# A hybrid conv/attention/mixture-of-experts block: the overflow table moved into the conditional block, twelve expert units in place of thirteen, and each unit's down projection one unit later

## The chip, the cores and the metric

The kernel runs on one core of a Trainium2 chip. The metric is the device time of one execution in microseconds (us); the figure to predict is the median of several runs. Besides those runs, one execution was profiled, and every row below comes from that one.

## The reference, cut to what matters

One layer on 512 tokens of width 1024, all in float32. The first half (convolution module, latent attention, output projection) is not touched by the change. The second half is a mixture of 32 experts; each token goes to two of them:

```
def hier_moe(h, w_group, b_group, w_expert, b_expert, w_gate_e, w_up_e, w_down_e):
    ...                                  # top group of 4, top 2 experts of its 8, weights "gates"
    y = jnp.zeros_like(h)
    for e in range(N_EXPERTS):           # 32; w_gate_e[e], w_up_e[e]: 1024 x 256, w_down_e[e]: 256 x 1024
        a = jax.nn.silu(h @ w_gate_e[e]) * (h @ w_up_e[e])
        y = y + gates[:, e:e + 1] * (a @ w_down_e[e])
    return y
```

Each expert has 3 MB of weights, so all 32 have 96 MB. The tokens that each expert gets follow from the inputs. Counted with the reference's own draw (seed 0), expert 5 has 87 tokens, the next four have 57, 53, 53 and 50, and 512 x 2 = 1024 rows are spread over the 32.

## The kernel before, in words

**Units.** The experts are worked off in units. A unit holds 128 rows of gathered tokens. The string `ORDER = "eeellsllsolss"` gives the sequence. An `e` unit has two experts fixed beforehand (experts 0 to 5 in three units), with 64 rows each. An `l` unit has two experts that are chosen at run time, by length, with 64 rows each; an `s` unit has four of the shorter ones with 32 rows each. The `o` unit has the first overflow: an expert with more tokens than rows is loaded again, for up to 64 more. Here expert 5 has 87 tokens and 64 rows, so its last 23 tokens are the `o` unit's. Further overflow would be worked off behind the units in nested conditional blocks (`over_body`, `nest`), which jump over their content when `n_over` is small.

**Tiles.** The weights of an expert come in three tiles of 1 MB: part 0 (half of the gate and up weights), part 1 (the other half), and part `d` (down). `load` issues them from SyncE's queue, in the order of the list `keys`: unit after unit, within a unit part 0 of all its experts, part 1, `d`. There are 33 x 3 = 99 tiles. `room` lists the free buffers: 4 of a ring (`r`) and 14 slots (`s`). So 18 tiles are loaded before the first unit runs; after that, each tile waits for a buffer that a unit gives back. SyncE's queue is in order: one tile whose buffer is not free holds all that come after it.

**A unit's steps.** `start` gathers the rows (an indirect DMA issued by POOL, two units ahead), transposes them on TensorE (L1443) and scales them. `gate_up` (L1467) multiplies by part 0 and then part 1. ACT and DVE make silu and product (L1470, L1472), `turn` transposes the result (L1479), `down` (L1492) multiplies by `d`; DVE scales with the routing weight (L1495), ACT rounds the high part (L1496), POOL takes the low part (L1497). `combine` (L1503, L1508) scatters the rows back to tokens by a matmul with a one-hot matrix (L1456) and adds them to the residual, for two units at once, eight groups of 512 columns by 128 tokens. The engines' orders are written out by hand: in each unit TensorE does `gate_up`, the next unit's transposes, part of a `combine`, `turn`, another part, `down`.

**Beside the units.** The first unit's rows are made without a gather, as a matmul (`first_unit`). Routing weights (`gates`) are computed behind the first unit's start. `scatter` then writes the overflow table to DRAM by eight indirect DMAs from POOL (L1319); `table` is filled beforehand. `over_table` makes the list of overflow blocks. The last unit's `part 1` and `d` tiles are cut in two and loaded alternately for two experts at a time.

Of the kernel before, what the change touches and what calls it, by code (L numbers as in the profile page):

```python
# [34 lines left out]
NSTAT, NLONG = 6, 10  # L35
# [5 lines left out]
def hybrid_block(ctx: ExitStack, tc: tile.TileContext, A, out, dbg=None, stop=None):  # L41
# [21 lines left out]
    NW, NSL = 4, 17  # L63
# [16 lines left out]
    tmp = ctx.enter_context(tc.tile_pool(name="tmp", bufs=6))  # L80
# [839 lines left out]
    ORDER = "eeellsllsolss"  # L920
# [47 lines left out]
    ahead, HOLD = [], 99  # L968
    UE, ULONG = NSTAT // 2, NLONG // 2
    UO = UE + ULONG + NSHORT // 4  # L970
    room = ["r"] * 4 + ["s"] * 14
# [5 lines left out]
    def load(key, n):  # L977

# [6 lines left out]
        if isinstance(e, int):  # L985
            pick = lambda w: w[e]
        else:
            if part == 0:
                src = oi[0:1, 0:1] if e is None else od[0:1, e[1]:e[1] + 1]
                reg_of[e] = sp.value_load(src, min_val=0, max_val=31)  # L990
            pick = lambda w: w[bass.ds(reg_of[e], 1)].rearrange("e p a b -> (e p) a b")
# [12 lines left out]
    def load_keys(ks):  # L1004

        first = len(Wt)
        for ds in zip(*[load(key, len(ks)) for key in ks]):
            for o, i in sum(ds, []):
                d = sp.dma_start(o, i)
                if first == HOLD:  # L1010
                    tc.add_manual_dep(d.ins, ahead[0].ins.name, sync, reason="order of the transfers")
                    first = None


    units = []
    keys = []
    for kind in ORDER:
        n_ = sum(k == kind for k, _, _ in units)
        if kind == "e":
            u_ = n_, [2 * n_, 2 * n_ + 1]  # L1020
        elif kind == "l":
            u_ = UE + n_, [("p", NSTAT + 2 * n_ + i) for i in range(2)]
        elif kind == "s":
            u_ = UE + ULONG + n_, [("p", NSTAT + NLONG + 4 * n_ + i) for i in range(4)]
        else:
            u_ = None, [None]
        ks = [[(e, part) for e in u_[1]] for part in (0, 1, "d")]
        keys += sum(ks if units else [ks[0], ks[2], ks[1]], [])
        units.append((kind, *u_))
    nxt = [0]  # L1030
    LAST = [(units[-1][2][i], part) for i in range(0, len(units[-1][2]), 2) for part in (1, "d")]

    def loads_upto(n):
        while room and nxt[0] < min(n, len(keys)):
            m = 2 if keys[nxt[0]] in LAST else 1
# [7 lines left out]
    rt = C([128, 2160], name="u", uname="rt")  # L1043
    rpos = [0]

    def R(shape, dt=F32):
# [5 lines left out]
        assert rpos[0] <= 2160  # L1052
# [34 lines left out]
    tfill = T([128, NROW // 128, 2])  # L1087
    dve.memset(tfill[:, :, 0], 1000.0)
    dve.memset(tfill[:, :, 1], 0.0)
    fill = pool.dma_start(table.rearrange("(p a) b -> p a b", p=128), tfill)  # L1090
    tokrow = R([512])
    iota(tokrow, [[1, 512]], 0)
    i4, i32, i64 = tokrow[:, :4], tokrow[:, :32], tokrow[:, :64]
# [9 lines left out]
    Vt = rt[:32, :128]  # L1103
    i32, e32 = tokrow[:, :32], tokrow[:32, :32]
    iota(ecol, [[0, 1]], 0, 1)
    dve.tensor_scalar(kbase[:, :NSTAT], e32[:, :NSTAT], -20000.0, 1e6, op0=OP.mult, op1=OP.add)
    dve.tensor_scalar(kbase[:, NSTAT:], e32[:, NSTAT:], -1.0, 31.0, op0=OP.mult, op1=OP.add)
# [39 lines left out]
    def route(tt):  # L1147
# [52 lines left out]
        dve.tensor_tensor(mr, M[:, 0, 0:2], M[:, 1, 0:2], op=OP.add)  # L1200
# [6 lines left out]
        dve.tensor_tensor(o, i64b, pk[:, 0:2, None].to_broadcast([128, 2, 64]), op=OP.is_equal)  # L1207
# [5 lines left out]
        hot = R([2, 64])  # L1213
        dve.tensor_tensor(hot, i64b, rk[:, :, None].to_broadcast([128, 2, 64]), op=OP.is_equal)
# [31 lines left out]
    def place(tt, o, r):  # L1246
# [4 lines left out]
        for k in range(2):  # L1251
            for h in range(2):
                pe.matmul(pst[0][64 * h:64 * h + 64, o:o + UE], hot[:, k, :], r[:, k, h:NSTAT:2],
# [3 lines left out]
    def by_expert(tt, o, r):  # L1257

        hot = routed[tt][-1]
        for k in range(2):  # L1260
            pe.matmul(pst[0][:32, 128 + o:192 + o], r[:, k, :], hot[:, k, :], start=False, stop=(tt == 3 and k == 1),
                      tile_position=(0, 0), skip_group_check=True)

    def by_unit(o):

        v = Vt[:, o:o + 64]
        for h in range(2):
            pe.matmul(pst[0][64 * h:64 * h + 64, 256 + o:256 + o + ULONG], v, perm[:, NSTAT + h:NSTAT + NLONG:2],
                      start=False, stop=True, tile_position=(0, 64 * h), skip_group_check=True)
        for i in range(4):  # L1270
            pe.matmul(pst[0][32 * i:32 * i + 32, 256 + o + ULONG:256 + o + UO - UE], v[:, :32], perm[:, NSTAT + NLONG + i::4],
                      start=False, stop=True, tile_position=(0, 32 * i), skip_group_check=True)

    def gates():
# [20 lines left out]

# [5 lines left out]
        for tt in range(4):  # L1301
            place(tt, 64, routed[tt][5])
            by_expert(tt, 64, routed[tt][5])
        dve.tensor_copy(sv[:, :UE, 1], pst[0][:, 64:64 + UE])
        dve.tensor_copy(Vt[:, 64:], pst[0][:32, 192:256])
        yield
        by_unit(64)
        dve.tensor_copy(sv[:, UE:UO, 1], pst[0][:, 320:320 + UO - UE])
        yield

    def rows_by_unit():
        by_unit(0)
        dve.tensor_scalar(sidx[:, UE:UO], pst[0][:, 256:256 + UO - UE], 1000.0, None, op0=OP.add)
        dve.tensor_scalar(sv[:, UE:UO, 0], pst[0][:, 256:256 + UO - UE], 1000.0, None, op0=OP.add)

    def scatter():
        for tt in range(4):
# [19 lines left out]
    for tt in range(4):  # L1337
# [5 lines left out]
        if tt < 3:  # L1343
            n = 31 + 8 * tt
            for d, f in ((0, lambda tt=tt: x2_part(tt, 1)), (D0, step), (D1, lambda step=step: step(2)), (D2 if tt < 2 else 8.5, step),
                         (D3 if tt < 2 else 11.5, places)):
                at(n + d, f)
    rows0 = chain(*[first_unit(tt) for tt in range(3)])
    last_rows = first_unit(3)
    for n, f in ((53, lambda: x2_part(3, 1)), (53, lambda: run(rows0, 2)), (55, lambda: x2_part(3, 2)), (55.1, step),  # L1350
                 (55.6, lambda: run(rows0, 1)), (55.8, step), (56, step), (56.1, lambda: run(rows0, 1)), (57, lambda: step(2)),
                 (58, lambda: run(rows0, 2)), (60, step), (61, lambda: run(last_rows)), (62, places)):
# [22 lines left out]
    dve.tensor_copy(Vt[:, :64], pst[0][:32, 128:192])  # L1375
# [4 lines left out]
    def over_table():  # L1380
        rpos[0] = 128
# [5 lines left out]
        dve.tensor_scalar(xn[:32, 4:5], place_of, NSTAT + NLONG - 0.5, 32.0, op0=OP.is_gt, op1=OP.mult)  # L1387
# [29 lines left out]
        ov = R([2 * NOVER + 1])  # L1417
        dve.tensor_copy(ov, pov[:, :2 * NOVER + 1])
        dve.tensor_scalar(ov[:, NOVER:2 * NOVER], ov[:, NOVER:2 * NOVER], NROW - 64.0, None, op0=OP.add)
        dve.tensor_copy(oi[:, :2 * NOVER + 1], ov)  # L1420
# [6 lines left out]
    class Unit:  # L1427
# [3 lines left out]
        def __init__(self, ne, tokf, gate, buf, weights, first=False):  # L1431
            self.ne, self.gate, self.buf, self.weights = ne, gate, buf, weights
            self.w = w = 32 if ne == 4 else 64
            n = self.n = w * ne
            self.hg = hg
            if first:
                act.copy(buf[:, :512], pg[0])
                dve.tensor_copy(buf[:, 512:], pg[1])
# [8 lines left out]
            self.rest = pt, tokf  # L1447

        def complete(self):
            pt, tokf = self.rest  # L1450
# [4 lines left out]
            self.ot = T((128, 512), F32R)  # L1455
            dve.tensor_scalar(self.ot[:n], tokrow[:n], tokf, None, op0=OP.is_equal)  # L1456

        def gate_up(self, between=None):
            n, wd_ = self.n, self.w
            gu = acc()  # L1460
            for j in range(8):
                if j == 4 and between:
                    between()
                for i in range(self.ne):
                    w = self.weights(i, j // 4)
                    sl = slice(wd_ * i, wd_ * i + wd_)
                    pe.matmul(gu[sl, :], self.hg[:, j, sl], w.t[:, :, j % 4, :],  # L1467
                              start=(j == 0), stop=(j == 7), tile_position=(0, wd_ * i), skip_group_check=True)
# [14 lines left out]
        def down(self, last=False):  # L1483
            n, wd_ = self.n, self.w
            self.yhl = S([128, 2, 1024], F32R)
            for hf in range(2):
                hs = slice(512 * hf, 512 * hf + 512)
                o = acc()
                for c in range(2):
                    for i in range(self.ne):  # L1490
                        w = self.weights(i, "d")
                        pe.matmul(o[wd_ * i:wd_ * i + wd_, :], self.aT[:, n * c + wd_ * i:n * c + wd_ * i + wd_], w.t[:, c, hs],  # L1492
                                  start=(c == 0), stop=(c == 1), tile_position=(0, wd_ * i), skip_group_check=True)
# [3 lines left out]
                (dve if last and hf else pool).tensor_tensor(self.yhl[:n, 1, hs], yf[:n], self.yhl[:n, 0, hs].bitcast(F32), op=OP.subtract)  # L1497

    def scattered(o, tt, hf, us, start, stop):

        for m, u_ in enumerate(us):
            for k in range(2):
                pe.matmul(o, u_.ot[:u_.n, tt * 128:(tt + 1) * 128], u_.yhl[:u_.n, k, 512 * hf:512 * hf + 512],  # L1503
                          start=start and m == 0 and k == 0, stop=stop and m == len(us) - 1 and k == 1)

    def add(o, tt, hf):
        xr = xrow(tt)[:, 512 * hf:512 * hf + 512]
        dve.tensor_tensor(xr, xr, o, op=OP.add)  # L1508
        return xr

    def combine(us):

        for tt in range(4):
            for hf in range(2):
                o = fb()
                scattered(o, tt, hf, us, True, True)
                add(o, tt, hf)
                yield

    def combine_last(before, last):  # L1520

        o = {}

        def first(tt, hf, bank):
            o[tt, hf] = bank()
            scattered(o[tt, hf], tt, hf, [before], True, False)

        for tt in (2, 3):
            first(tt, 0, fb)
            yield  # L1530
        for tt in (0, 1):
            first(tt, 0, acc)
        for hf in range(2):
            for tt in (2, 3, 0, 1):
                if hf:
                    first(tt, 1, acc if tt > 1 else fb)
# [212 lines left out]
```

## Time and profile before

| | us |
|---|---|
| median of 3 runs | 569.61 |
| lowest and highest | 567.05 and 572.83 |
| the profiled execution's own time | 565.29 |
| its span, first to last instruction | 563.7 |
| TensorE busy in the span | 495.8 |
| VectorE (DVE), ScalarE (ACT), GpSimd (POOL) busy | 301.8, 201.5, 182.4 |
| first matmul of the first unit | 302.91 |

The profiled execution is 4.3 us below the median. Busy shares are averages over stages with different limits: up to about 300 us TensorE and DVE work at the first half of the layer, and from there on the expert units run. The rows below are of that second stage.

### The profile page before, as it was taken

To read this page: it belongs to the slowest core of one execution; us is meant where nothing else is said; L and a number is where in the kernel's file an instruction comes from. 1 tells how busy PE (TensorE), PEld (TensorE's weight loads), DVE (VectorE), ACT (ScalarE), POOL (GpSimd) and SP (SyncE) were. 2 spreads that over 40 slices of the span, in tenths; PEclk is the share of its full clock that TensorE was granted. 3 is DMA by queue.
4 is the path that set the end of the run, shared out by engine and by line. 5 is a ranking of instruction groups with operands and counts; after the bars stand their busy time and mean duration, and the time that the engine had idled before them with its cause. 6 is when DMAs were issued, how large, how long until landed. Compare 5 with 4: busy or idle time off the path is not lost.

```text
span 563.7 us, 8250 instructions
## 1 busy us (share of the span) xinstructions
PE 495.8 (88%) x2845; PEld 284.3 (50%) x2845; DVE 301.8 (54%) x645; ACT 201.5 (36%) x427; POOL 182.4 (32%) x161
## 2 busy tenths in 40 slices
PE   4999999948997888999998699999999799998674
PEld 3778865525642455788863333344444145433123
DVE  2457699998978675642655214544444034355014
ACT  4234745435687566722444121222222021112000
POOL 3110666957789543000012521222122111111000
PEclk9999999968999999999999689999999889999898
DMA  8999445846950244287785669999999999999974
GB/s 250 304 347 280 165 172 221 358 151 194 246 192 0 76 149 131 106 308 247 275 334 199 212 222 323 406 380 414 413 398 409 413 415 412 405 417 404 317 274 157
DMA packets 60931, 156.36 MB, mean 277 GB/s; under 512 B 7805, under 2 KB 27405, under 8 KB 55120
## 3 DMA queue, kind: packets, MB, share of 16 engines
q1 hardware_dynamic: 57280, 149.06, 73.3%
q0 software_dynamic: 2208, 4.18, 2.4%
q10 hardware_dynamic: 1392, 2.51, 1.2%
q8 instruction: 25, 0.41, 0.3%
q14 instruction: 26, 0.21, 0.1%
HBM read 153.25 MB, written 4.63 MB: 280 GB/s over the span
## 4 chain that ended last, share of the span: by engine, by line
PE 44%; DMA 18%; DVE 8%; ACT 3%; another core or an unknown queue 2%; issue 1%; POOL 1%; DVEq 0%; ACTq 0%
PE acc L1467 12%; DMA s<-in_w_down_e_dram 7%; PE acc L1492 6%; DMA s<-in_w_up_e_dram 6%; PE f L1503 5%; PE acc L116 3%; PE acc L118 2%; PE acc L117 2%; DMA w<-in_w_ada_dram 2%; DVE sm L877 2%; PE acc L876 1%; PE tr L1443 1%; DVE sm L878 1%; DMA xg<-t 1%; PE acc L908 1%
## 5 line engine op out<-in xcount | busy, mean ns | idle before, releaser
L1467 PE MATMUL acc<-s,gw 128*64 128x512 f32 (+1 forms) x368 | 84.5, 633 | 7.1 <-DMA s<-in_w_up_e_dram 7.1
L116 PE MATMUL acc<-s,s 128*128 128x512 f32 (+3 forms) x160 | 64.7, 405 | 10.2 <-DVE s L317 8.2
L1497 POOL TENSOR_TENSOR s<-t,s 128x512 fp32r<-128x512 f32 (+1 forms) x25 | 31.8, 1274 | 123.4 <-ACT s L1496 102.1
L344 DVE SCALAR_TENSOR_TENSOR dw<-s,cwh,dw 128x512 f32<-128x512 f32 x60 | 63.3, 1055 | 1.5
L118 PE MATMUL acc<-s,s 128*128 128x512 f32 (+3 forms) x160 | 60.3, 377 | 1.1 <-DVE s L378 1.1
L117 PE MATMUL acc<-s,s 128*128 128x512 f32 (+3 forms) x160 | 60.1, 376 | 0.0
L1472 DVE TENSOR_TENSOR t<-t,acc 128x256 f32<-128x256 f32 (+1 forms) x13 | 5.5, 420 | 92.6 <-ACT t L1470 92.6
L1503 PE MATMUL f<-s,t 128*128 128x512 f32 (+1 forms) x192 | 53.0, 410 | 2.1 <-DVE s L1508 2.1
L1467 PEld LDWEIGHTS acc<-s,gw 128*64 128x64 f32 (+1 forms) x368 | 23.1, 128 | 54.6 <-issue 51.6
L1508 DVE TENSOR_TENSOR s<-s,f 128x512 f32<-128x512 f32 x60 | 39.2, 681 | 19.9 <-PE f L1503 19.9
L356 POOL TENSOR_TENSOR dw<-dw,s 128x512 f32<-128x512 f32 x30 | 45.5, 1518 | 13.1 <-ACT s L354 11.4
L1467 PE MATMUL acc<-w,gw 128*64 128x512 f32 (+1 forms) x160 | 45.9, 616 | 3.3 <-DMA w<-in_w_up_e_dram 3.2
L1492 PE MATMUL acc<-s,t 128*64 128x512 f32 (+1 forms) x200 | 46.2, 598 | 2.1 <-DMA s<-in_w_down_e_dram 2.0
L116 PEld LDWEIGHTS acc<-s,s 128*128 128x128 f32 x160 | 31.2, 195 | 24.4 <-DVE s L317 8.6
L1496 ACT CAST s<-t 128x512 fp32r<-128x512 f32 (+1 forms) x26 | 16.1, 618 | 75.7 <-DVE t L1495 75.7
L1503 PEld LDWEIGHTS f<-s,t 128*128 128x128 f32 (+1 forms) x192 | 33.5, 188 | 15.3 <-DVE s L1508 3.6
L1470 ACT ACTIVATE t<-acc 128x256 f32<-128x256 f32 (+1 forms) x13 | 5.0, 384 | 100.9 <-PE acc L1467 100.9
L118 PEld LDWEIGHTS acc<-s,s 128*128 128x128 f32 x160 | 31.1, 194 | 5.6 <-DVE s L378 1.5
L1495 DVE SCALAR_TENSOR_TENSOR t<-acc,rt,gw 128x512 f32<-128x512 f32 x24 | 18.0, 750 | 29.4 <-PE acc L1492 29.4
L1424 POOL DMA_INDIRECT s<-xg,sidx x11 | 11.5, 1047 | 67.7 <-PE tr L1443 37.8
L117 PEld LDWEIGHTS acc<-s,s 128*128 128x128 f32 x160 | 31.3, 195 | 3.4 <-issue 0.2
L354 ACT ACTIVATE s<-s,cwh 128x512 f32<-128x512 f32 x30 | 21.5, 719 | 14.5 <-POOL dw L356 14.3
(323 smaller groups left out, 870.5 us busy)
## 6 DMA issues: line engine op xcount, KB each, us to landing
s<-in_w_down_e_dram SPq DMA_DIRECT2D x23, 1024.0 KB
s<-in_w_gate_e_dram SPq DMA_DIRECT2D x44, 512.0 KB
s<-in_w_up_e_dram SPq DMA_DIRECT2D x44, 512.0 KB
w<-in_w_ada_dram SPq DMA_DIRECT2D x16, 1024.0 KB
w<-in_w_gate_e_dram SPq DMA_DIRECT2D x18, 512.0 KB
w<-in_w_up_e_dram SPq DMA_DIRECT2D x18, 512.0 KB
s<-in_w_ada_dram SPq DMA_DIRECT2D x6, 1024.0 KB
w<-in_w_down_e_dram SPq DMA_DIRECT2D x6, 1024.0 KB
```

The costliest lines, as they stand in the source:

```text
L116: pe.matmul(o, lh, rh, start=start, stop=False)
L117: pe.matmul(o, lh, rl, start=False, stop=False)
L118: pe.matmul(o, ll, rh, start=False, stop=stop)
L344: dve.scalar_tensor_tensor(dw[:, t, :], u[:, t, k:k + 512], w, dw[:, t, :], op0=OP.mult, op1=OP.add)
L354: act.activation(z[k % 2], u[:, t, k:k + 512], AF.Copy, scale=cwh[:, 31 * t + k:31 * t + k + 1])
L356: pool.tensor_tensor(dw[:, t, :], dw[:, t, :], z[(k - 1) % 2], op=OP.add)
L1467: pe.matmul(gu[sl, :], self.hg[:, j, sl], w.t[:, :, j % 4, :], start=(j == 0), stop=(j == 7), tile_position=(0, wd_ * i), skip_group_check ...
L1492: pe.matmul(o[wd_ * i:wd_ * i + wd_, :], self.aT[:, n * c + wd_ * i:n * c + wd_ * i + wd_], w.t[:, c, hs], start=(c == 0), stop=(c == 1), ...
L1495: dve.scalar_tensor_tensor(yf[:n], o[:n], self.gate, gf[:n, hs], op0=OP.mult, op1=OP.mult)
L1497: (dve if last and hf else pool).tensor_tensor(self.yhl[:n, 1, hs], yf[:n], self.yhl[:n, 0, hs].bitcast(F32), op=OP.subtract)
L1503: pe.matmul(o, u_.ot[:u_.n, tt * 128:(tt + 1) * 128], u_.yhl[:u_.n, k, 512 * hf:512 * hf + 512], start=start and m == 0 and k == 0, stop=s ...
L1508: dve.tensor_tensor(xr, xr, o, op=OP.add)
```

## The change

- `scatter`, with the filling of `table`, moves into `over_body(0)`, so it is issued only when there is overflow; `nest` starts at 0, and the `o` unit is gone, with its load of one expert and its read of the table.
- There are 12 units: `ORDER = "eeellsllsxss"`. The new `x` unit has the longest of the run-time experts with 96 rows (64 and 32) and one of the shorter ones with 32. `PIECES` lists which rows of a unit go to which expert. The one-hot matrices for placing tokens are 96 wide instead of 64, and 9 experts instead of 10 count as long. The fixed experts are 0, 1, 2, 24, 25, 26, so expert 5 is now chosen at run time and falls to the `x` unit.
- `down` of a unit runs one unit later, behind the next unit's `gate_up` and the transposes of the one after. A unit's `d` buffers are given back one unit later too.
- `combine` always takes the sums of two units, four groups in each unit, first the left 512 columns and then the right ones, and makes its one-hot matrices when it begins. The unit before the last is combined alone, within the last unit's `gate_up`; the last unit's `down` and `combine` alternate by halves of the columns, with the stores.
- `room` has one slot more (15), so 19 tiles are loaded early. There are 18 slots instead of 17 and 7 temporary buffers instead of 6; POOL's DMA descriptor space is set to 4096 bytes.
- The last unit's tiles are all cut in two: parts 0 and 1 for two experts at a time, `d` for four at a time.
- Smaller moves: `gates` is finished after the second unit's `gate_up` instead of the first's; `rows_by_unit` runs behind the first unit's `gate_up` instead of in its middle; the first unit's rows are copied out of PSUM before the ordering of the experts; `gb`, the buffer of the gathered rows, is taken and cleared before the routing.

```
-NSTAT, NLONG = 6, 10
+EARLY = slice(0, 3), slice(24, 27)
+NSTAT, NLONG = 6, 9
...
-    NW, NSL = 4, 17
+    NW, NSL = 4, 18
...
-    ORDER = "eeellsllsolss"
+    ORDER = "eeellsllsxss"
...
-    room = ["r"] * 4 + ["s"] * 14
+    room = ["r"] * 4 + ["s"] * 15
...
+    PIECES = {2: [(0, 64, 0), (64, 64, 1)], 4: [(32 * i, 32, i) for i in range(4)],
+              "x": [(0, 64, 0), (64, 32, 0), (96, 32, 1)], 1: [(0, 64, 0)]}
...
-    LAST = [(units[-1][2][i], part) for i in range(0, len(units[-1][2]), 2) for part in (1, "d")]
+    LAST = {(units[-1][2][0], "d"): 4}
+    LAST.update({(units[-1][2][i], part): 2 for i in (0, 2) for part in (0, 1)})
...
+    gb = S([128, 2, 1024])
+    pool.memset(gb, 0.0)
...
     for n_ in range(len(units)):
-        last = len(units) - 1 - n_
-        K = COMB[2 if SOLO <= n_ else n_ % 2] if last else (0, 1, 1, 0)
-        cur.gate_up(lambda: (run(comb, K[0]), n_ or rows_by_unit()))
-        if n_ == 0:
-            run(gate, 1)
-            scatter()
+        last = n_ == len(units) - 1
+        if last:
+            run(comb)
+            run(prev.down())
+            comb = combine([prev])
+        cur.gate_up(lambda: last and run(comb))
+        if n_ == 1:
+            run(gate)
         nxt_u = start(n_ + 1)
...
         if nxt_u:
             nxt_u.complete()
-        if n_ == 0:
-            run(gate)
+        if last:
+            cur.turn()
+            down, comb = cur.down(dve), combine([cur], (fb, fb, tr, tr), True)
+            for hf in range(2):
+                run(down, 1)
+                run(comb, 4)
+            break
+        if prev:
+            run(prev.down())
+            done.append(prev)
         cur.turn()
-        run(comb, K[2])
-        cur.down(not last)
-        run(comb, K[3])
...
+        if len(done) == 2:
+            comb, done = combine(done), []
+        run(comb, 4)
...
-        r_ = [Wt[e, part].room for part in (0, 1, "d") for e in units[n_][2]]
+        r_ = [Wt[e, part].room for part in (0, 1) for e in units[n_][2]]
         if n_ < 3:
             r_.remove("s")
+        if n_:
+            r_ += [Wt[e, "d"].room for e in units[n_ - 1][2]]
...
     def over_body(k):
+        if k == 0:
+            scatter()
...
-    nest(1)
+    nest(0)
```

## Rows read from the trace of the kernel before

**Rows 1.** Stretches: start:end, length, busy time per engine, granted clock, DMA share, GB/s
```profile
300.00:306.00 6.00, 4.79 (x29) 2.89 (x30) 3.46 (x18) 3.57 (x11) 2.33 (x2) 1.00 0.22 57
306.00:312.00 6.00, 5.76 (x55) 2.45 (x52) 3.60 (x22) 2.85 (x10) 2.58 (x3) 1.00 0.77 238
312.00:320.00 8.00, 4.38 (x36) 2.94 (x34) 0.00 (x0) 0.00 (x0) 5.33 (x6) 0.61 0.73 277
320.00:330.00 10.00, 8.65 (x38) 3.09 (x40) 3.54 (x8) 2.96 (x7) 2.31 (x2) 0.63 0.20 50
330.00:345.00 15.00, 13.60 (x65) 5.33 (x63) 6.54 (x15) 3.04 (x8) 3.29 (x4) 1.00 0.97 368
345.00:365.00 20.00, 18.77 (x90) 7.20 (x88) 7.75 (x23) 4.12 (x9) 5.31 (x5) 1.00 0.97 355
...
440.00:520.00 80.00, 74.37 (x377) 30.58 (x370) 31.28 (x52) 13.62 (x32) 11.80 (x11) 0.96 1.02 412
520.00:530.00 10.00, 5.57 (x35) 1.27 (x33) 0.29 (x1) 0.00 (x0) 1.10 (x1) 1.00 0.92 305
```
**Rows 2.** SyncE's queue in order of time: start, length of the issue, transfer
```profile
306.58 0.36 SPq L1009 DMA_DIRECT2D w<-in_w_gate_e_dram  x1
...
311.18 0.51 SPq L1009 DMA_DIRECT2D s<-in_w_up_e_dram  x1
328.70 0.33 SPq L1009 DMA_DIRECT2D w<-in_w_gate_e_dram  x1
```
**Rows 3.** The chain of waits from the first unit on: start, length, what
```profile
302.91 3.73 PE acc L1467 x16
...
311.48 9.01 another core or an unknown queue
...
322.63 6.05 PE acc L1492 x16
...
335.54 1.02 PE tr L1443 x8
...
340.67 3.58 PE acc L1492 x16
```
**Rows 4.** Instructions around the second unit's start: start, length, idle time before
```profile
314.58 0.48 PE L1261 MATMUL f<-rt 128*32 128x64 f32 x3 [0.99 <-issue]
...
317.87 0.98 POOL L1319 DMA_INDIRECT table<-rt,ridx  x1 [0.30 <-issue]
...
320.52 0.16 DVE L1304 COPY rt<-f 128x3 f32<-128x3 f32 x1 [9.03 <-remote]
...
328.51 7.03 PE L1467 MATMUL acc<-s,gw 128*64 128x512 f32 x32
```
**Rows 5.** The chain of waits at the end
```profile
546.91 1.90 PE acc L1492 x10
...
554.16 1.89 DVE s L1508 x3
...
556.39 0.25 DVE s L1508
```
**Rows 6.** Groups of instructions, 365 to 440 us: count, busy, mean ns
```profile
L1503 PE MATMUL f<-s,t 128*128 128x512 f32 x80 | 20.9, 405 | 0.0
...
L1456 DVE TENSOR_SCALAR t<-rt 128x512 fp32r<-128x512 f32 x5 | 2.4, 479 | 0.0
```
**Rows 7.** DVE in order of time, behind the last tile
```profile
548.92 0.75 DVE L1495 SCALAR_TENSOR_TENSOR t<-acc,rt,gw 128x512 f32<-128x512 f32 x1 [1.94 <-PE acc L1492]
550.36 0.69 DVE L1497 TENSOR_TENSOR s<-t,s 128x512 fp32r<-128x512 f32 x1 [0.69 <-ACT s L1496]
```
**Rows 8.** A stretch with waits for tiles, columns as in the first group
```profile
447.00:453.80 6.80, 5.86 (x26) 1.30 (x25) 0.00 (x0) 0.00 (x0) 0.00 (x0) 0.50 1.02 423
```
**Rows 9.** POOL: the clearing of gb; below it the four roots of the second norm
```profile
291.05 1.81 POOL L1552 MEMSET s<- 128x2048 f32 x1
...
L193 POOL TENSOR_TENSOR rt<-sm,nhalf x4: 548/551/568, 266.8 to 290.6; 128x1 f32<-128x1 f32 x4
```

More of the change, by code (lines that the diff above doesn't have):

```diff
@@ L1004, in load_keys @@
     def load_keys(ks):
[L1006 to L1007 removed]
+        for ds in zip(*[load(key, min(len(ks), 2)) for key in ks]):
             for o, i in sum(ds, []):
[L1009 to L1012, printed above, removed]
+                sp.dma_start(o, i)
+    PIECES = {2: [(0, 64, 0), (64, 64, 1)], 4: [(32 * i, 32, i) for i in range(4)],
+              "x": [(0, 64, 0), (64, 32, 0), (96, 32, 1)], 1: [(0, 64, 0)]}
     units = []
@@ L1294, in gates @@
             dve.tensor_tensor(rh, M, valv[:, tt, :, 1:2].to_broadcast([128, 2, 32]), op=OP.mult)
+        yield
+        for tt in range(4):
+            place(tt, 64, routed[tt][5])
+            by_expert(tt, 96, routed[tt][5])
+        dve.tensor_copy(sv[:, :UE, 1], pst[0][:, 64:64 + UE])
+        dve.tensor_copy(Vt[:, 96:], pst[0][:32, 224:320])
+        yield
+        by_unit(1)
+        dve.tensor_copy(sv[:, UE:UO, 1], pst[0][:, 336:336 + UO - UE])
+        for tt in range(4):
+            L, m8, e8, j8, M, rh, rk, hot = routed[tt]
             rx = ov[:, tt, :]
@@ L1506, in add @@
[L1506 to L1517, printed above, removed]
-                yield
[L1520 to L1532, printed above, removed]
-        for hf in range(2):
-            for tt in (2, 3, 0, 1):
-                if hf:
-                    first(tt, 1, acc if tt > 1 else fb)
-            for tt in (2, 3, 0, 1):
-                scattered(o[tt, hf], tt, hf, [last], False, True)
-                sp.dma_start(out[0, tt * 128:(tt + 1) * 128, 512 * hf:512 * hf + 512], add(o[tt, hf], tt, hf))
@@ L1541, in over_rows, with combine @@
-    def over_rows(k, reg):
-        ot_ = small(2, tag="ovt", bufs=2)
-        oix = small(1, I32, tag="ovi", bufs=2)
-        d = pool.dma_start(ot_[:64], table[bass.ds(reg, 64)])
+                eng.tensor_tensor(self.yhl[:n, 1, hs], yf[:n], self.yhl[:n, 0, hs].bitcast(F32), op=OP.subtract)
+                yield
+    def combine(us, banks=None, store=False):
+        for u_ in us:
+            u_.one_hot()
+        for hf in range(2):
+            for tt in range(4):
+                o = banks[tt]() if banks else fb()
+                for m, u_ in enumerate(us):
+                    for k in range(2):
+                        pe.matmul(o, u_.ot[:u_.n, tt * 128:(tt + 1) * 128], u_.yhl[:u_.n, k, 512 * hf:512 * hf + 512],
+                                  start=(m == 0 and k == 0), stop=(m == len(us) - 1 and k == 1))
+                xr = xrow(tt)[:, 512 * hf:512 * hf + 512]
+                dve.tensor_tensor(xr, xr, o, op=OP.add)
+                if store:
+                    sp.dma_start(out[0, tt * 128:(tt + 1) * 128, 512 * hf:512 * hf + 512], xr)
+                yield
@@ L1546, in over_rows, with table_rows @@
+    def table_rows(o, reg, n):
+        d = pool.dma_start(o, table[bass.ds(reg, n)])
         for o in scat:
             tc.add_manual_dep(d.ins, o.ins.name, sync, reason="table")
-        return ot_, oix
-    gb = S([128, 2, 1024])
     hg = ga.rearrange("p (j q) -> p j q", j=8)
-    clear = pool.memset(gb, 0.0)
-    tc.add_manual_dep(clear.ins, roots[-1].ins.name, nosync, reason="off the routing's way")
     rows_of = {}
@@ L1657, in over_body @@
         u_.turn()
-        u_.down()
+        run(u_.down())
         run(combine([u_]))
```

196 lines of the change are left out of this document (83 added, 113 removed).

## The prediction

> **What bounds the kernel now.** I read the page's two lines of slices first, then a table by stretch, then SyncE's queue, and last the engines around the one hole that the table shows. Behind 345 us the DMA share is 0.97 or more up to 520 us, at about 410 GB/s where nothing holds it [rows 1]: the stage is paced by the arrival of weight tiles. TensorE looks full there as well, but its wait comes last only in places. What decides is therefore how many tiles come behind the first unit, how long DMA stands still before the steady stream begins, and the tail behind the last tile. The early stretches show the standstill: the DMA share is 0.22, 0.77, 0.73 and 0.20 between 300 and 330 us. The idle part of each stretch is its length times one minus the share: 4.7 + 1.4 + 2.2 + 8.0, then 0.5 and 0.6 to 365 us, in all 17.3 us.
>
> [...] TensorE's last placing matmul is recorded at 314.58, POOL's last scatter is issued at 317.87, DVE goes on at 320.52 [rows 4]. The rows don't say whether the eight scatters hold the chain or the burst of small matmuls does.
>
> **The price of a tile.** The first of the 81 late tiles is issued at 306.58 and the last has landed at 546.91, where the chain turns to the last matmuls [rows 2, 5]: 240.3 us. Take off the standstills in that time (1.4 + 2.2 + 8.0 + 0.5 + 0.6 and 0.8 from 520 to 530, 13.4 us). Take off the slower small pieces: 305 GB/s at a share of 0.92 is 332 per busy time, against 412 / 1.02 = 404 [rows 1], so 1.049 MB takes 3.16 instead of 2.60 us, 0.56 more; eight tiles are cut so, 4.5 us. The rest, 222.4 us for 81 tiles, is 2.75 us each, gathers and waits for buffers included.
>
> **The change part by part.**
>
> *Fewer tiles.* The overflow unit's three go, and a 19th is loaded early, in time that stands idle from 300 to 306. Of 81 late tiles 77 stay: -4 x 2.75 = -11.0 us. The bounds are 2.60 and 2.75: -10.4 to -11.0. That nothing takes the overflow unit's place follows from the counts: 87 fits in 96 rows, the eight next (57 to 31) in 64, all other run-time experts have at most 30 for 32 rows, and the fixed ones at most 50. So the block that makes the table is jumped over.
>
> *The standstill.* Now the first unit's `gate_up` begins at 302.91 [rows 3]. The earlier copy out of PSUM takes about 0.7 us off its way, the wider one-hots give back 0.2 or so: I take 302.2. Its halves (7.03 / 2 [rows 4]) end at 305.8 and 309.2 and give back two tiles and one. DMA stands from 304 (the 19th tile done) to 305.8, 1.8 us, then works to 314.0. TensorE: transposes 1.02 [rows 3], the placing matmuls and `turn` about 1.5, so the second `gate_up` begins near 312 instead of 328.51 [rows 4], and gives back two tiles at 315.6 (1.6 us of standstill), one at 319.1. They last to 323.8. Then come the burst for the routing weights (some 4 us), transposes, and the late `down` (3.58 [rows 3]): two tiles at 328, 4.2 us of standstill. The third `gate_up`, from 328.5, and the second late `down` feed DMA to 347; the fourth one's first half comes about 2 us late. Sum 9.6, with 1.5 us for handovers 11.1, against 17.3: -6.2 us. Bounds: 0 if the later `down` takes the depth that it gives (its two to four buffers are held one unit longer, and SyncE's queue holds all behind them), and -10 if the third standstill hides.
>
> *Scatter and table.* Eight issues leave POOL (0.98 each; nobody behind them but one gather [rows 4]), and their landing leaves DMA. Off the path that the last paragraph already counts, this is nothing; it adds nothing later, since POOL's cover is its idle time. If the hold is the burst's, it comes back behind the second `gate_up`: 320.5 - 315.1 = 5.4 us, from 0 to +5.4. I take 0, as the scatter's end is the nearest in time to the release.
>
> *The last unit in smaller pieces.* Twelve tiles instead of eight are cut: +4 x 0.56 = +2.3 us (0 to 2.3). [...]
>
> *TensorE's new order.* Per unit it has the same work: 7.03 + 1.02 + 3.58 + about 0.5, and a group of four scatter matmuls is 4 x 0.405 less their overlap, 0.93 [rows 3, 4, 6], four in a unit. New is a wait at each `combine`'s begin: DVE makes two one-hots (0.48 each [rows 6]) behind the second eviction of `down` (0.75 [rows 7]), and TensorE stands some 1.2 us, with the next `gate_up` queued behind it. Five times that is 6 us of TensorE, which costs nothing while it leads DMA: it is 16 us earlier than before at the third unit. The cover is gone if the lead is less than 6 us; then up to +6.
>
> *The tail.* Before, from 546.91 to the end of the last add at 556.64 is 9.7 us: 1.9 of matmuls, 2.2 of eviction, rounding and subtraction [rows 7], then scatter matmuls for all eight groups and the adds, 0.63 each [rows 5]. Afterwards the left columns are done while the right half of `d` lands: 1.9 + 2.2 + 0.5 + 4 x 0.63, with handovers 6.9. So -2.8 us (0 to -4). The 7 us from there to the span's end (stores, the jump) stay.
>
> The sum is -11.0 - 6.2 + 2.3 - 2.8 = -17.7 us. The profiled execution had 565.3 us, so a like one would have 547.6; the median of the runs lies 4.3 above it, and from 569.6 the same sum gives **551.9 us**.
>
> **The rivals.**
>
> *The hold comes back* (5.4 us behind the second `gate_up`). For it: TensorE's records have gaps from 313 on, and the burst grows by half. Against it: the release follows the last scatter. 551.9 + 5.4 = 557.3.
>
> *TensorE becomes the bound*, by the one-hot waits, or the late buffers keep the standstill. Either takes back some 6 us: 558. For it: TensorE is busy 18.8 of 20 us from 345 to 365 [rows 1]. Against it: its lead of 16 us.
>
> [...]
>
> *The stream runs freer than I take it.* The 2.75 us hold waits for buffers; one more slot and an earlier release may bring it to 2.60: 77 x 0.15 = -11.5, 540.4.
>
> *Slower: the clearing of `gb`.* It takes 1.81 us on POOL, at 291 behind all four roots [rows 9]. It now stands ahead of them in POOL's order, and its slot may still belong to a tile of the output projection. If so, the first root (266.8) waits, and with it the routing and the first unit. If the slot comes free as late as the last slot before (about 291), the start is 24 us late: 569.6 - 17.7 + 24 = 576. It decides from a delay of 18 us. Against it: POOL idles long before 266.8, and with 18 slots one is spare when the routing begins.
>
> *It doesn't do what it says:* if other inputs are run, the overflow block is taken, with three tiles (8 us) and a unit alone: over 590.
>
> **How the numbers follow.** Chances: forecast 0.45, hold 0.18, TensorE's bound or kept standstill 0.11, cool tail 0.06, freer stream 0.13, clearing 0.05, overflow 0.02. The range reaches from the freer stream with a hidden third standstill (540.4 less some 3, 537) to the hold and TensorE's bound together (551.9 + 5.4 + 6 = 563.3, say 564). One per cent, 5.7 us, is about what a measurement of this kernel tells from no change. All cases but the last two give over that; as two of them can meet, with a shorter gain from the tail, I take 0.07 off: faster 0.86, within one per cent 0.08, slower 0.06.
>
> **What would show it.** In the profile after: the second `gate_up` near 312 us; no issue gap in SyncE's queue over 6 us; a DMA share over 0.5 from 320 to 330; last tile landed near 532; from there to the last add some 7 us. I am wrong if the tiles come at more than 2.8 us each, if the 9 us hold is still there, or if the first `gate_up` isn't by 303.

## The result and the profile after

The changed kernel takes 549.52 us in the median of four runs (546.79 to 550.6); the kernel before, run beside it, takes 568.33 (564.06 to 572.83). The ratio is 0.9686, with a 95% interval from 0.9613 to 0.976: faster by about 3%. Some executions are slower (in e10, below, one of 548.09 us, at a granted clock of 0.956, where the median is 542.53), and the ratios and intervals leave those out. The prediction said 551.9. The profiled execution had 550.6 us with a span of 549.0, against 565.3 and 563.7.

The stretches of the kernel after, with the columns of [rows 1]: start:end, length, busy time of PE, PEld, DVE, ACT and POOL, granted clock, DMA share, GB/s.

```profile
300.00:306.00 6.00, 5.61 (x32) 3.38 (x34) 2.79 (x16) 4.30 (x15) 2.17 (x2) 1.00 0.70 237
306.00:312.00 6.00, 5.37 (x44) 2.95 (x42) 2.59 (x12) 3.64 (x10) 0.62 (x1) 1.00 0.93 333
312.00:320.00 8.00, 8.00 (x54) 3.25 (x55) 0.93 (x2) 0.74 (x2) 0.37 (x1) 1.00 0.98 350
320.00:330.00 10.00, 9.60 (x74) 5.03 (x74) 4.93 (x19) 2.12 (x5) 1.99 (x2) 0.83 0.77 300
330.00:345.00 15.00, 13.94 (x68) 5.83 (x65) 5.18 (x10) 4.29 (x10) 5.27 (x6) 1.00 0.98 359
345.00:365.00 20.00, 20.00 (x95) 9.05 (x95) 8.81 (x19) 3.40 (x8) 3.58 (x3) 1.00 0.99 363
365.00:400.00 35.00, 33.88 (x192) 14.69 (x190) 14.80 (x32) 6.79 (x16) 7.21 (x6) 1.00 1.02 399
...
500.00:510.00 10.00, 10.00 (x59) 5.76 (x61) 6.16 (x9) 0.00 (x0) 0.92 (x1) 1.00 0.99 328
510.00:520.00 10.00, 9.19 (x60) 3.58 (x52) 5.55 (x10) 1.24 (x2) 2.57 (x2) 1.00 0.94 320
...
531.00:535.00 4.00, 4.00 (x19) 1.85 (x21) 2.67 (x4) 0.00 (x0) 0.00 (x0) 0.57 0.53 197
```

The idle part of DMA from 300 to 365 us is 1.8 + 0.4 + 0.2 + 2.3 + 0.3 + 0.2 = 5.2 us; before it was 17.3 [rows 1]. SyncE's queue and TensorE, the kernel after, in order of time (start, length):

```profile
305.86 0.34 SPq L1008 DMA_DIRECT2D w<-in_w_gate_e_dram  x1
...
319.55 0.34 SPq L1008 DMA_DIRECT2D s<-in_w_up_e_dram  x1
329.20 0.34 SPq L1008 DMA_DIRECT2D w<-in_w_gate_e_dram  x1
```
```profile
302.18 3.72 PE L1480 MATMUL acc<-w,gw 128*64 128x512 f32 x16
...
311.88 7.09 PE L1480 MATMUL acc<-s,gw 128*64 128x512 f32 x32
...
321.41 0.52 PE L1258 MATMUL f<-rt 128*32 128x96 f32 x4
322.33 0.60 PE L1267 MATMUL f<-rt 32*64 32x4 f32 x16 [0.40 <-DVE rt L1302]
322.86 1.76 PE L1454 MATMUL tr<-ident,s 128*128 128x128 f32 x8
324.56 4.62 PE L1506 MATMUL acc<-w,t 128*64 128x512 f32 x16
```

The second `gate_up` begins at 311.88, where it began at 328.51 before [rows 4]. The burst of small matmuls ends at 321.9, and the next work follows after 0.4 us: the 9 us of [rows 3, 4], the hold, are gone. Before, SyncE's queue went on 0.02 us behind the end of the first `down` [rows 2, 3], which came behind the hold and ran at a granted clock of 0.60. SyncE's longest gap between weight tiles is still 9.6 us (319.55 to 329.20), for 17.5 [rows 2], but it costs 2.3 us of DMA only, since tiles that had been issued earlier were still on their way.

The chain that ended last, the kernel after, the pieces on TensorE at the end:

```profile
475.26 10.12 DMA w<-in_w_up_e_dram
...
490.13 7.99 PE acc L1506 x24
...
499.35 8.07 PE f L1523 x32
...
525.78 1.97 PE acc L1506 x16
...
530.45 1.31 PE f L1523 x4
531.75 1.71 PE tr L1523 x4
533.46 2.58 PE acc L1506 x16
...
538.86 1.89 DVE s L1526 x3
```

Behind 485.4 no transfer stands in this chain any more. Before, a transfer stood in it until the last tile was in, right ahead of the first piece of [rows 5]:

```profile
536.20 10.66 DMA s<-in_w_down_e_dram
```

So at the end TensorE's order is the bound, which the prediction had as a rival for the whole stage. The last tile is in at 530.3, but the last `down` half begins at 533.46, behind the scatter matmuls of the left columns.

For the profiled executions below, e8's left out, the same four times in us. The last tile is where the weights' queue has moved all its bytes but the 2.1 MB of the output, worked out from the packets of the trace. The start of the first `gate_up` varies by 5 us from work ahead of the change, so the last three columns count from there.

| kernel | first gate_up | last tile | last add | span's end |
|---|---|---|---|---|
| before | 302.9 | +243.4 | +253.7 | +260.8 |
| before, again (e12) | 306.4 | +242.0 | +252.5 | +259.2 |
| after | 302.2 | +228.1 | +239.2 | +246.8 |
| after, again (e11) | 301.5 | +224.8 | +237.2 | +244.1 |
| e1, equal widths | 305.7 | +227.2 | +236.4 | +243.9 |
| e2, last down first | 303.5 | +227.0 | +238.6 | +245.6 |
| e3, fewer cuts | 301.3 | +221.5 | +237.1 | +244.7 |
| e4, scatters back | 304.7 | +234.3 | +246.3 | +252.7 |
| e5, before without overflow unit | 305.5 | +228.1 | +240.0 | +246.9 |
| e6, and without scatters | 305.8 | +225.9 | +236.4 | +243.4 |
| e7, 18 early | 305.9 | +226.8 | +238.8 | +246.5 |
| e9, four edits | 302.4 | +220.9 | +230.9 | +239.3 |
| e10, three edits | 301.3 | +222.3 | +232.3 | +239.0 |

### The profile page after: what moved, and what is told of

The parts are those of the page before. It is cut to its first block, busy times and chain, and to the rows that moved or that the text cites. A ratio compares the mean times of both kernels' runs of the same rounds, so it can differ in the third digit from the quotient of the medians.

```text
span 549.0 us, 8137 instructions
## 1 busy us (share of the span) xinstructions
PE 486.6 (89%) x2827; PEld 277.8 (51%) x2827; DVE 298.5 (54%) x631; ACT 197.3 (36%) x419; POOL 169.2 (31%) x147
## 4 chain that ended last, share of the span: by engine, by line
PE 46%; DVE 23%; DMA 20%; ACT 3%; SPq 3%; issue 2%; POOL 1%; ACTq 0%; DVEq 0%; POOLq 0%
DVE dw L345 10%; PE acc L1480 10%; DMA s<-in_w_up_e_dram 9%; PE acc L1506 6%; PE f L1523 5%; DMA w<-in_w_up_e_dram 4%; PE acc L117 4%; PE acc L119 3%; PE acc L118 3%; DMA w<-in_w_down_e_dram 3%; DMA s<-in_w_down_e_dram 2%; DMA s<-in_w_ada_dram 2%; PE acc L909 2%; DVE sm L879 2%; PE acc L877 1%
## 5 line engine op out<-in xcount | busy, mean ns | idle before, releaser
L1480 PE MATMUL acc<-s,gw 128*32 128x512 f32 (+1 forms) x392 | 93.3, 604 | 1.5 <-DMA s<-in_w_up_e_dram 1.5
L1523 PE MATMUL f<-s,t 128*128 128x512 f32 x184 | 48.7, 412 | 10.8 <-DVE t L1462 8.1
L1480 PE MATMUL acc<-w,gw 128*32 128x512 f32 (+1 forms) x136 | 53.5, 619 | 4.1 <-DMA w<-in_w_up_e_dram 4.0
L1485 DVE TENSOR_TENSOR t<-t,acc 128x256 f32<-128x256 f32 x12 | 5.1, 421 | 91.0 <-ACT t L1483 91.0
L1511 POOL TENSOR_TENSOR s<-t,s 128x512 fp32r<-128x512 f32 x22 | 28.5, 1295 | 75.9 <-ACT s L1510 75.9
L1480 PEld LDWEIGHTS acc<-s,gw 128*32 128x32 f32 (+1 forms) x392 | 25.8, 123 | 47.9 <-issue 46.4
L1506 PE MATMUL acc<-s,t 128*32 128x512 f32 (+1 forms) x200 | 45.3, 609 | 0.5 <-ACT t L1494 0.5
L1523 PEld LDWEIGHTS f<-s,t 128*128 128x128 f32 x184 | 31.1, 188 | 26.9 <-DVE s L1526 7.3
L1510 ACT CAST s<-t 128x512 fp32r<-128x512 f32 x24 | 14.8, 618 | 54.8 <-DVE t L1509 54.8
L881 ACT ACTIVATE t<-acc,sm,qs 128x128 f32<-128x128 f32 (+3 forms) x32 | 19.7, 616 | 19.9 <-DVE sm L879 16.6
```

The costliest lines, as they stand in the source:

```text
L881: act.activation(e[:, :n], p[:, :n], AF.Exp, scale=qs[:, qt, h:h + 1], bias=H["nb"][:, qt:qt + 1], accum_out=H["rs"][:, qt:qt + 1])
L1506: pe.matmul(o[o_:o_ + w_, :], self.aT[:, n * c + o_:n * c + o_ + w_], w.t[:, c, hs], start=(c == 0), stop=(c == 1), tile_position=(0, o_), ...
L1511: eng.tensor_tensor(self.yhl[:n, 1, hs], yf[:n], self.yhl[:n, 0, hs].bitcast(F32), op=OP.subtract)
```

## The experiments

They ran in three groups of four (e1 to e4, e5 to e8, e9 to e12). The changed kernel itself stood beside them in the third group only (e11). The kernel before, beside them, had 567.85, 561.9 and 567.34 us. That is a spread of 1% for one kernel, so times are compared within a group, and across groups only where more than that is at stake.

**e1: equal widths in the mixed unit.** Mixed pieces are a 64-column one beside two of 32.

```
-"x": [(0, 64, 0), (64, 32, 0), (96, 32, 1)]
+"x": [(32 * i, 32, i // 3) for i in range(4)]
```

> The mixed unit (96 rows of one expert, 32 of another) keeps its rows and tiles, but the 96 rows are worked off as three pieces of 32 columns instead of one of 64 and one of 32. Theory A (two widths don't run side by side on TensorE, and its order is what bounds the last two units): that unit's down falls from 8.0 to 3.7 us and its gate_up from 16.0 to about 7.5; the last unit's second gate_up half ends about 3 us earlier, where the arrival of its tiles stops it, so the time falls by about 3 us. Theory B (the arrival of tiles bounds up to the last one, as the prediction has it): the two durations fall the same way, but the time changes by less than 1 us. If the widths aren't the cause, the down stays at 8 us.

548.63 us (546.87 to 551.14), ratio 0.9671 [0.9631, 0.971]. One line of the kernel after, then one of e1: the mixed unit's `down` (matmuls, count, nanoseconds, forms; in e1 the first number is its start and the second its length).

```profile
L1506 PE MATMUL acc<-s,t x24: 592/604/643, 490.1 to 497.5; 128*32 128x512 f32 x16, 128*64 128x512 f32 x8
```
```profile
493.65 3.64 PE L1506 MATMUL acc<-s,t 128*32 128x512 f32 x32
```

More matmuls (32 for 24) of about the same length (median 592 for 604 ns) take 3.64 instead of 8.0 us; `gate_up` falls from 15.95 to 8.9, of which 0.8 is a wait for a tile. In the kernel after the pieces of 64 and of 32 run one behind the other, while equal ones run side by side: in `gate_up`, after begins six matmuls every 1.98 us, e1 four of about 0.6 us every 0.43. From the mixed `gate_up` of the kernel after:

```profile
456.26 0.59 PE L1480 MATMUL acc<-s,gw 128*32 128x512 f32 x1
456.27 0.59 PE L1480 MATMUL acc<-w,gw 128*32 128x512 f32 x1
456.79 1.62 PE L1480 MATMUL acc<-s,gw 128*64 128x512 f32 x3
```

The two of 32 columns start together, and the next of 64 starts when they are about done (456.85); its x3 takes in one of 32 columns at its end. Why TensorE takes the two widths in turn was not shown. From the first `gate_up` the span is 3 us shorter than in the first profile of after, but equal to the second; the time alone can't be told from the changed kernel's. That the mixed widths make the `down` long is shown (8.0 us for 3.64); what that alone adds to the time is not.

**e2: both halves of the last `down` first.**

```
-for hf in range(2):
-    run(down, 1)
-    run(comb, 4)
+run(down, 2)
+run(comb, 8)
```

> Of the last unit both halves of down go ahead of the scatter matmuls in TensorE's order. The prediction's term (tail of 6.9 us instead of 9.7 behind the last tile) fell because the right half stands behind the left columns' scatter matmuls: if so, the right half ends near 532 instead of 536, and the time falls by 2 to 3 us. Rival (the order of the halves is right, since the left columns' adds then come late and in one row of eight): the time stays within 1 us or grows.

551.84 us, ratio 0.971 [0.9661, 0.9759]. From the last tile to the last add it is 11.6 us, as in after (11.1, 12.4). The right half ends sooner (533.0, from 536.0), but then all eight groups of scatter matmuls and adds come behind it. The rival held: the order of the halves was not the fault.

**e3: gate and up tiles of the last unit whole again.**

```
 LAST = {(units[-1][2][0], "d"): 4}
-LAST.update({(units[-1][2][i], part): 2 for i in (0, 2) for part in (0, 1)})
```

> The last unit's eight gate and up tiles come whole again; only its four d tiles are cut. The prediction prices a cut tile at 0.56 us, so the last tile should land 4.5 us earlier, near 525.5. Theory A (TensorE's order bounds the last two units): the time falls by at most 2 us, since the second gate_up half ends at 523.8 either way. Theory B (the arrival of tiles bounds): it falls by 4 to 5 us. If small pieces cost nothing, the last tile still lands at 530.

549.98 us (0.9693 [0.9641, 0.9744]). Two stretches of e3, mostly whole tiles in the first and the last unit's cut `d` tiles in the second; then the first of these stretches in e11, the changed kernel run again, with cut tiles:

```profile
500.00:510.00 10.00, 10.00 (x71) 4.56 (x73) 5.87 (x9) 1.24 (x2) 1.61 (x2) 1.00 1.03 408
510.00:520.00 10.00, 9.17 (x60) 3.61 (x56) 5.14 (x8) 0.00 (x0) 0.96 (x1) 1.00 1.01 376
```
```profile
500.00:510.00 10.00, 10.00 (x72) 4.74 (x74) 6.09 (x9) 1.24 (x2) 1.36 (x2) 1.00 1.03 373
```

408 GB/s for whole tiles stand against 328 in the first profile of after and 373 in the second: cut tiles are slower in both, but by how much differs between two executions of one kernel. The last tile is in 3.3 to 6.6 us earlier for eight tiles, 0.4 to 0.8 us each. The last add follows 15.6 us later instead of 11.1 or 12.4: TensorE takes nearly all of it. Theory A holds.

**e4: fill and scatters put back, in the second unit.**

```
 if n_ == 1:
     run(gate)
+    scatter()
...
-        if k == 0:               # in over_body
-            scatter()
```

> The fill of the overflow table and the eight scatters are put back behind the routing weights' matmuls of the second unit, though nobody reads the table here. Theory S (the scatters are what held the chain for 9 us before): DVE and TensorE stand for 5 to 9 us behind 322, the third gate_up begins near 336 instead of 329.5, the stretch 320 to 340 loses 4 to 8 us of DMA, and the time grows by 3 to 6 us. Rival (the burst of small matmuls held it, or its gathers): the third gate_up stays within 2 us and the time within 1 us.

559.07 us, ratio 0.9851 [0.981, 0.9891]: 7 to 10 us more than its three neighbours, and more than I expected. But the place was another one. The third `gate_up` was as early as in after (27.4 us behind the first); the hold came while the scatters ran on, one unit later. Instructions of e4, POOL and then DVE:

```profile
341.87 0.98 POOL L1326 DMA_INDIRECT table<-rt,ridx  x1 [0.30 <-issue]
```
```profile
339.68 0.42 DVE L1485 TENSOR_TENSOR t<-t,acc 128x256 f32<-128x256 f32 x1 [7.05 <-issue]
345.57 0.69 DVE L1468 TENSOR_TENSOR gw<-tr,G 128x512 f32<-128x512 f32 x1 [5.47 <-remote]
...
347.22 1.40 DVE L1509 SCALAR_TENSOR_TENSOR t<-acc,rt,gw 128x512 f32<-128x512 f32 x2
```

DVE waits 5.47 us for transposes that TensorE's records have done by 340.2, until behind the last scatter; `turn` and `combine` follow late, and DMA's share falls to 0.84 and 0.85 from 330 to 365. So filling the table and scattering costs time here, clear of noise; which of the two, and by what path, this run doesn't tell apart.

**e5 and e6: the kernel before without its overflow unit; then without the scatters too.** Both leave 23 rows of one expert out of the output.

```
-ORDER = "eeellsllsolss"
+ORDER = "eeellsllslss"          # e5 and e6
-    scatter()                   # e6: fill and scatters only in the conditional block
```

> The kernel before without the overflow unit's place in the order: three tiles and one unit fewer, everything else as before, scatters included (23 rows of one expert are left out of the output). The prediction's price of 2.75 us for a tile gives -8.2 us, near 559.7. Rival (TensorE's order bounds the end, as in the changed kernel): the unit's own work on TensorE, some 7 us of matmuls and 4 of scatter matmuls, counts as well, and the time falls by more than 10 us; or the three tiles were hidden, and it falls by less than 4.

553.96 us against 561.9 beside it, ratio 0.988 [0.982, 0.9941]: -7.9 us, where three tiles at 2.75 make -8.2. That agrees with the price, and leaves nothing for the unit's own work on TensorE. It doesn't show the price: e5's profile has no hold (below), its last tile comes 14 to 15 us earlier than in the two profiles of the kernel before, and no profile tells how many of the 17 executions beside it (554.87 to 568.55 us) had the hold.

> The same without overflow unit, and the fill of the table and the eight scatters are made only in the conditional block (as in the changed kernel); the burst of small matmuls stays behind the first gate_up. Theory S (the scatters hold the chain): the 9 us of DVE and ACT behind 311 are gone, the first down begins near 314 instead of 322.6, and the time falls by another 6 to 9 us, to 551 to 554. Rival (the burst holds it): the gap stays over 5 us and the time within 1.5 us of the run without overflow unit.

551.84 us (0.9867 [0.9805, 0.9928]), 2 us below e5 and not to be told from it. The likely reason is in e5's one profile: it has the scatters and no hold. e6 has the burst of small matmuls in its old place, without scatters, and no hold either, so the burst alone doesn't make one. DVE in e5, and then DVE and the last scatter in e12, the unedited kernel before:

```profile
314.65 0.42 DVE L1472 TENSOR_TENSOR t<-t,acc 128x256 f32<-128x256 f32 x1 [1.46 <-ACT t L1470]
316.76 0.16 DVE L1304 COPY rt<-f 128x3 f32<-128x3 f32 x1 [1.69 <-PE f L1261]
```
```profile
315.10 0.42 DVE L1472 TENSOR_TENSOR t<-t,acc 128x256 f32<-128x256 f32 x1 [0.93 <-ACT t L1470]
323.69 0.16 DVE L1304 COPY rt<-f 128x3 f32<-128x3 f32 x1 [8.17 <-PE tr L1443]
```
```profile
321.25 0.98 POOL L1319 DMA_INDIRECT table<-rt,ridx  x1 [0.30 <-issue]
```

The same instruction waits 1.69 us in e5 and 8.17 in e12, with eight scatters behind the first `gate_up` in both.

**e7: one slot held back, 18 tiles early.**

```
-room = ["r"] * 4 + ["s"] * 15
+room = ["r"] * 4 + ["s"] * 14
...
-if n_ < 3:
+if n_ in (1, 2):                 # the held slot is given out behind the first unit
```

> The changed kernel with one slot held back until the first unit's end, so that 18 tiles are loaded early instead of 19. The prediction's price of a tile gives +2.75 us, near 552.2, with the last tile landing near 532.5. Rival (the first units' standstill of DMA takes the tile in either way): within 1 us, and the stretch 300 to 306 loses half of its 0.70 while 306 to 320 stays full.

551.38 us (547.29 to 556.19; 0.9828 [0.9766, 0.989]); the last tile is in at +226.8, between the two profiles of after. Two stretches of e7:

```profile
306.00:312.00 6.00, 6.00 (x22) 2.38 (x24) 2.83 (x17) 5.42 (x17) 2.40 (x2) 0.74 0.30 82
...
320.00:330.00 10.00, 9.60 (x96) 5.41 (x94) 2.23 (x14) 1.48 (x5) 0.48 (x1) 1.00 1.01 383
```

DMA stands 4.2 us in the first and none in the second, where after stands 2.3. (The first `gate_up` is 3.7 us later here, so the same work lies later in these stretches.) The standstill moves, and the profile shows no price of 2.75 us. The times don't settle it: 551.38 is 1.0 and 1.9 us above the changed kernel in its two groups, and by ratio to the kernel before, which was faster in this group, over 1% above it.

**e8: each `down` in its own turn, with the burst of routing weights behind the first `gate_up`.**

```
-    run(prev.down())             # ahead of turn
...
 cur.turn()
+run(comb, 4)
+run(cur.down())
```

> The changed kernel with each unit's down in its own turn again; the routing weights' burst, which the first down needs, goes with it behind the first gate_up. Theory L (the late down is what took the standstill from 17 to 5 us, by letting the second gate_up go first): the second gate_up begins some 8 us later, near 320, DMA stands for 4 to 8 us more between 306 and 330, and the time grows by 3 to 6 us. Rival (the scatters' absence alone did it, and the late down only keeps its buffers longer): the second gate_up begins later as well, but the first d buffers come back one unit earlier, and the time stays within 1.5 us.

558.13 us (0.9962 [0.9926, 0.9998]), 6.8 above e7 of the same group: a little over the 3 to 6 us of theory L, and far from the rival's 1.5. Its profiled execution took 564.53, 6.4 above the median, so its durations aren't compared. Its order can be read: the second `gate_up` begins 21.9 us behind the first (327.47 and 305.62), where it is 9.7 in after, since it stands behind the burst and the first `down` again. The edit moves the burst, the scatter matmuls and the return of the `d` buffers as well, and the run doesn't tell these apart.

**e9 to e12: the edits together, and both kernels again.** e9 is e1, e2 and e3 together, with the one-hots ahead of the evictions; e10 is the same without e2's edit.

```
 if prev:
+    for u_ in done + [prev] if done else ():
+        u_.one_hot()            # was: at combine's begin
     run(prev.down())
```

> The changed kernel with four edits together: the mixed unit's 96 rows as three pieces of 32, only the last unit's d tiles cut, each one-hot made ahead of its down's evictions, and both halves of the last down ahead of the scatter matmuls. Counted from the first gate_up, the last tile landed at 228 us and the last add ended at 239 us in the changed kernel; alone, the first edit gave 227 and 236, the second 221.5 and 237. Theory A (two bounds close together: the tiles' arrival and TensorE's order, so that an edit of one is stopped by the other): both together give 221 and 229 to 231, and the time falls by 6 to 9 us against the changed kernel run beside it. Rival (the edits' gains are the same two or three us): 235 or later, and the time falls by 2 to 4 us.

543.67 us (542.58 to 547.19), ratio 0.9615 [0.9569, 0.9661].

> The same without the last edit: the left columns' scatter matmuls stand ahead of the right half of down again. With the left half of d landed 6 us before the right one and TensorE no longer late, the left columns should now be done when the right half lands, as the prediction had it: a tail of 7 to 8 us from the last tile to the last add, and a time within 1.5 us of the run with the edit. If TensorE still comes late, it is 2 to 3 us slower than that run.

542.53 us (538.95 to 548.09), ratio 0.9572 [0.9515, 0.963].

> The changed kernel unedited, on the same chip as the two runs before it: last tile at 228 and last add at 239 us from the first gate_up, ratio to the kernel before between 0.965 and 0.985 (what stands beside it sets the gain: where the kernel before shows no hold, the gain is 7 to 8 us smaller).

550.38 us (547.22 to 552.21), ratio 0.972 [0.9675, 0.9766].

> The kernel before, unedited, for one more profile: if the hold behind the scatters belongs to every execution, DVE stands for some 9 us near 312 to 321 again, and the last tile lands near 243 us from the first gate_up. If it comes and goes, as the run without overflow unit suggests, DVE goes on behind 313 within 3 us and the last tile lands near 236.

567.31 us; the hold is there (8.17 us, above), and the last tile lands at +242.0.

So e9 and e10 are 6.7 and 7.9 us faster than the changed kernel beside them, where none of e1, e2 and e3 alone could be told from it. Both beat both kernels, and can't be told from each other. Two bounds close together fit this: the last tile comes as early as in e3, and now the last add follows (230.9 and 232.3, for 237.1 in e3). But the earlier one-hots never ran alone. What TensorE waited for ahead of the scatter matmuls, from the pages of after and of e10 (count, busy time, mean ns, idle time before them and what ended most of it):

```profile
L1523 PE MATMUL f<-s,t 128*128 128x512 f32 x184 | 48.7, 412 | 10.8 <-DVE t L1462 8.1
```
```profile
L1520 PE MATMUL f<-s,t 128*128 128x512 f32 x184 | 50.7, 418 | 6.3 <-ACT s L1509 3.1
```

L1462 makes the one-hots. TensorE waited 8.1 us for them in after, and in e10 for nothing more than 3.1. So how the gain divides between them, the equal widths and the whole tiles stays open.

e10's tail is not the 7 to 8 us expected. The chain of e10 at the end, and a stretch of it (columns as in [rows 1]):

```profile
523.57 0.96 PE f L1520 x3
524.53 0.93 PE tr L1520 x4
525.46 1.92 PE acc L1505 x16
...
529.66 1.58 PE f L1520 x3
531.23 1.72 PE tr L1520 x4
...
532.98 0.69 DVE s L1523
```
```profile
529.60:533.70 4.10, 3.28 (x7) 2.08 (x7) 2.75 (x5) 0.00 (x0) 0.00 (x0) 0.58 0.24 81
```

The last tile is in at 523.6. TensorE still finishes the left columns (1.8 us). From 527.4 to 529.66 it has next to nothing to do, and then the last scatter matmuls run at a granted clock of 0.58: 1.58 and 1.72 us, where the left columns' took 0.96 and 0.93. That makes 10.1 us in all.

## Why the prediction was right, point by point

*The sum, -17.7,* is borne out less well than the medians suggest. Counted from the first `gate_up`, the two pairs of profiles (before and after, e12 and e11) give -14.0 and -15.1 us, for -17.7 in the sum: the last tile -15.3 and -17.2, for -14.9, the tail +0.8 and +1.9, for -2.8, and 0.5 and 0.2 behind the last add. The rest of the medians' -18.8 lies ahead of the first `gate_up`, which came 0.7 and 4.9 us earlier, or in the scatter of the runs. So that 551.9 lies 2.4 us from 549.52 is luck in part.

*The price of a tile* held: 77 late tiles from 305.86 to 530.3 us, less 4.1 us of standstill (3.4 up to 365, 0.7 from 500 to 520) and twelve times 0.56, make 2.77 us each, for 2.75.

*Fewer tiles, -11.0.* For the overflow unit's three, e5 agrees (-7.9) but can't tell them from the hold. For the 19th, e7 doesn't settle a price. Here the sum counted twice: the 19th tile was to fill idle time between 300 and 306, and the same idle time was taken off again in the standstill (4.7 to 1.8). In truth the first late tile is issued only 0.7 us earlier.

*The standstill, -6.2,* is the mis-sized term: 17.3 went to 5.2, not to 11.1. The late buffers came nearly when I said (315.56 for 315.6, 318.99 for 319.1, 329.20 for 328). But the tiles ahead of them lasted longer than the 2.6 us each that I took: 350 to 363 GB/s at a share of 0.98 and 0.99 from 312 to 320 and from 330 to 365, against 399 from 365 to 400 (and 412 in [rows 1]). So part of this gain is only idle time turned into slow busy time. Why they were slower there, no run took apart. The double count and the standstill that was put too high take each other off in part, which is luck too: the last tile came at 530.3 for 532.

*The hold, 0.* Right: no hold in either profile of after. e4 prices the table's fill and the scatters in the changed kernel at 7 to 10 us, and e8 shows about as much (6.8) for the late `down` and what moves with it; the two can't be added to the rest, since each moves the same early standstill.

*Smaller pieces, +2.3.* The price per tile held in the stream (0.4 to 0.8 for 0.56): cut tiles, with runs of 2 KB, moved at 328 and 373 GB/s, whole tiles at 408. That a cut tile costs the stream nothing, the lower end of the bounds, no run shows. In the time it is nothing in the changed kernel (e3), since TensorE comes last there; together with equal widths and earlier one-hots the earlier last tile reaches the end.

*TensorE's new order, 0.* The step that said "per unit it has the same work" failed for the mixed unit: 15.95 + 8.0 us for 7.1 + 3.65. The waits for one-hots, put at 6 us, were 8.1. The cover of 16 us was there at the third unit (329.5 for 344.3 before) and used up at the end, from 485 on. The rival "TensorE becomes the bound" thus came true for the last two units. Its price doesn't show by itself, since e1 alone gains nothing that can be measured; e9 and e10 put it and the cut tiles together at 6.7 to 7.9 us.

*The tail, -2.8,* had the wrong sign: 11.1 and 12.4 us from the last tile to the last add, for 10.3 and 10.5 before (before, e12). Its own terms also add up to 7.1 us, not 6.9. I took the right half of `d` as waiting for its tile alone; it waits for the left columns' scatter matmuls (e2: another order only moves that wait), and TensorE then runs at a granted clock of 0.57 around it (531 to 535; 0.50 in [rows 8]). That is the cool tail of the chances, which gave it 0.06; the matmuls took 0.6 us more in that half of `down` (2.58 for 1.97) and about 0.9 more in the eight scatter matmuls ahead of it (3.02, where e10's left columns took 1.89 for seven).

*The clearing of `gb`* didn't delay the roots: it ran on POOL at 233.78, 33 us ahead of the first of them (266.73), and the first `gate_up` came at 302.18 and 301.5.

Of the signs, the second `gate_up`, the share from 320 to 330 (0.77), the first `gate_up` and the last tile came as forecast; the gap in SyncE's queue (9.6 us) and the tail (11.1 us) did not.

## What to carry to other kernels

Where two bounds lie close together (arrival of data and one engine's order), an edit of either can show nothing by itself, as e1 and e3 did; try them together before they are called worthless. When an edit fills idle time, price it once: either as work that no longer stands in the stream, or as idle time gone. A unit with a new shape gets its own price, from a run of that shape, even where its count of matmuls falls.

## What the runs showed of the hardware

Matmuls on column tiles of 64 and of 32 did not run side by side: 24 mixed ones took 8.0 us, 32 equal ones 3.64 (after, e1).

Eight scatters of eight-byte rows ran in four of the profiles. In three of them DVE, waiting for TensorE, stood for 9.03, 8.17 and 5.47 us (before, e12, e4), until 2.65, 2.44 and 3.70 us behind the begin of the last issue. By TensorE's records the burst's last matmul had ended 5.5 and 4.2 us earlier (before, e12), the transposes 5.4 us earlier (e4). In the fourth, e5, they ran with no such wait (1.69 us). In after and e6, without scatters, DVE's only waits over 4 us from 306 to 345 were for a whole `gate_up` (6.95 and 7.05 us; 6.6). What decides it stays open; it isn't which chip it was, since e5 and e12 ran on the same one.

Whole tiles moved at 408 GB/s and cut ones, with runs of 2 KB, at 328 and 373, at shares of 1.03, 0.99 and 1.03 (e3, after, e11).
